# Where the split weights start in their SBUF buffers: byte 128 of a 256-byte period for loaded and narrow tiles

## The chip, the cores and the metric

The kernel runs on one core of a Trainium2 chip. The metric is the device time of one launch in microseconds. Several runs are made and their median is taken; one further execution is recorded by the hardware profiler.

## What is computed

Two layers of an encoder on 256 tokens of width 2048, all in float32. Each layer is a projection with windowed attention and a bidirectional mLSTM behind it, an output projection, and an MLP with a squared ReLU, with RMSNorms around them:

```python
def hybrid_layer(x, ...):
    h = rms_norm(x, g_pre_mix)
    proj = h @ w_in                                   # 2048 x 4624
    aq, ak, av, mq, mk, mv, mo, mg = split(proj)
    att = window_attention(aq, ak, av, attn_sink)     # 8 heads of 128, 2 kv heads
    mem = mlstm_mixer(mq, mk, mv, mo, mg, conv_w, gate_bias, ml_norm_g)
    mix = concatenate([att, mem], axis=-1) @ w_out    # 2048 x 2048
    x = x + rms_norm(mix, g_post_mix)
    h = rms_norm(x, g_pre_mlp)
    u = square(relu(h @ w_up))                        # 2048 x 8192
    x = x + rms_norm(u @ w_down, g_post_mlp)          # 8192 x 2048
    return x
```

Nearly all arithmetic is in the four weight matrices of a layer.

## The kernel before

Every large product is made of three matmuls in the type float32r. Both operands are split into a high part (rounded by ScalarE) and the remainder (VectorE), and the sum is high x high, high x low and low x high. The tokens lie transposed: a tile of `tpool` (names `hT`, `h2T`, `uT`, `attT`, `memT`) holds 8 contraction blocks of 128, each with its high and its low part for 256 tokens, so 2048 bytes a block and partition, 1024 bytes a part.

The weights come from HBM in pieces of 1 MB at most (`load`, line 168). SP issues the DMA into `raw` (line 190), ScalarE makes `whi` (line 191), VectorE makes `wlo` (line 192). `whi` and `wlo` are tiles of the pool `wsp`, four buffers each, of 2048 + 64 elements of four bytes a partition, that is 8448 bytes, 33 times 256. Line 183 sets `o1`, the element of the buffer at which the piece starts.

The weight tiles of a layer are worked off in the order of `STAGES`: ten column tiles of the input projection ("in", widths 512, 512, 512, 272, five of 512, and 256), four of the output projection ("out"), then four blocks (`b` = 0 to 3) of four "up" and four "down" tiles, all 512 columns wide. While a tile is computed, the next one is loaded. There are two ways to compute a tile:

- `mm_k` (line 196), streamed weights: a 128 x 128 block of the tokens is loaded into TensorE as the stationary operand, and 512 (or 272, or 256) columns of weights stream through it. A piece holds four contraction blocks of the tile's width, one behind the other. This is the way of all "in", "out" and "down" tiles and of the first "up" tile of a layer.
- `mm_stationary` (line 259), loaded weights: a 128 x 128 block of weights is loaded, and the 256 tokens of `h2T` stream through it. A piece holds 16 contraction blocks of 128 columns. This is the way of the other 15 "up" tiles of a layer; each is 4 pieces x 16 blocks x 3 matmuls = 192 pairs of a weight load and a matmul. The result is written into the PSUM tile `mms`. The first block of a layer (`b` = 0) has three such tiles in a row, the others four.

TensorE takes its instructions in program order. Between the matmuls of the input projection stand the transposes and small matmuls of attention and mLSTM, which generators hand out one step after each contraction block (`pump`, line 210).

Where things lie in SBUF, as the built program has it (bytes in a partition): the pool `edge` with the 128 and 1024 bytes ahead of it ends at 2048; the four buffers of `tpool` start at 2048, 18432, 34816 and 51200; the buffers of `whi` at 67584, 76032, 84480 and 92928; those of `wlo` at 101376, 109824, 118272 and 126720. All of these are multiples of 256, and so are the starts of all parts in the token tiles. With `o1 = 16` a stationary piece starts 64 bytes behind a multiple of 256; with `o1 = 0` a streamed piece starts at one. The contraction blocks of a stationary piece are 512 bytes long, those of the 512-wide tiles 2048, of the 256-wide tile 1024 and of the 272-wide tile 1088.

Of the kernel before, what the change touches and what calls it, by code (L numbers as in the profile page):

```python
# [75 lines left out]
def stationary(key):  # L76


    _, st, b, n = key
    return st == "up" and (b, n) != (0, 0)  # L80
# [6 lines left out]
def encoder_kernel(ctx, tc, x, wall, rope, conv_w, gate_bias, ml_g, sink, gpre, gpost, out):  # L87
# [70 lines left out]
    order = []  # L158
# [9 lines left out]
    def load(i, begin=None):  # L168


        if i >= len(order) or order[i] in pieces:
            return
        o, w = offs[order[i]]
        k, n = (KC, P) if stationary(order[i]) else (PK, w)
        got = []
        for q in range(NPC):
            raw = wraw.tile([P, k, n], F32, tag="raw", name="raw")
            a = o + q * P * k * n
            src = wall[a:a + P * k * n].rearrange("(p k n) -> p k n", p=P, k=k)
            if begin is not None:  # L180
                begin(q)

            o1 = 16 if stationary(order[i]) else 0
            hi, lo = (
                wsp.tile([P, 2048 + 64], F32R, tag=x, name=f"w{x}")[:, o1:o1 + k * n].rearrange(
                    "p (k n) -> p k n", k=k) for x in ("hi", "lo"))
            step = 1 if begin is not None and q < 2 else k
            for j in range(0, k, step):
                sl = slice(j, j + step)
                nc.sync.dma_start(raw[:, sl], src[:, sl])  # L190
                nc.scalar.activation(hi[:, sl], raw[:, sl], AF.Copy)  # L191
                nc.vector.tensor_tensor(out=lo[:, sl], in0=raw[:, sl], in1=hi[:, sl].bitcast(F32), op=ALU.subtract)  # L192
            got.append((hi, lo))
        pieces[order[i]] = got
# [25 lines left out]
    def mm_tile(key, T, stages=(), after=None, at=None, half=False):  # L220

        load(pos[key])
        load(pos[key] + 1)
        if stages:
            ps = [psmm.tile([P, NT, 512], F32, tag="mm", name="mm")[:, 0] for _ in range(NT)]
# [30 lines left out]
    def mm_stationary(key, T, after):  # L259

        load(pos[key])
        load(pos[key] + 1)
        for pair in range(2):
            both = psmm.tile([P, 2, 512], F32, tag="mm", name="mms")
            ps = both[:, 0].rearrange("p (i t) -> p i t", i=2)
            for i in range(2):
                hi, lo = pieces[key][2 * pair + i]
                for k in range(KC):  # L270
                    Tk = T[k // 8][:, k % 8]
                    nc.tensor.matmul(ps[:, i], lhsT=hi[:, k], rhs=Tk[:, 0], start=(k == 0), stop=False)  # L272
                    nc.tensor.matmul(ps[:, i], lhsT=hi[:, k], rhs=Tk[:, 1], start=False, stop=False)  # L273
                    nc.tensor.matmul(ps[:, i], lhsT=lo[:, k], rhs=Tk[:, 0], start=False, stop=(k == KC - 1))  # L274
            after(pair, ps)
# [369 lines left out]
    def begin(q):  # L645
        if q:
            load_x(1, q - 1)
            load_x(0, q)
# [310 lines left out]
```

## Time and profile before

| | us |
|---|---|
| median of 3 runs | 2143.5 |
| lowest and highest | 2141.52, 2146.43 |
| the profiled execution | 2146.89 |
| its span, first to last instruction | 2145.1 |
| TensorE matmul busy | 2110.1 (98%) |
| TensorE weight load busy | 1868.9 (87%) |
| VectorE busy | 1134.4 (53%) |
| ScalarE busy | 983.8 (46%) |
| GpSimd busy | 60.4 (3%) |

The span is what lies between the first and the last instruction on the chip; the execution's own time has some 2 us around it. Matmuls are pipelined: one starts before the one ahead of it has ended, and the recorded duration of one is longer than what it adds to the time. What it adds is read from the starts in the timeline.

### The profile page before, as it was taken

The numbers are of one execution on the slowest core, as the hardware profiler recorded it, in microseconds if no ns is written. First come the engines' busy times: TensorE is split into PE (matmuls) and PEld (weight loads), VectorE is DVE, ScalarE is ACT, GpSimd is POOL, SyncE is SP. The second block draws the span as 40 slices with busy tenths as digits, with TensorE's granted clock in tenths as the row PEclk, the third lists the DMA queues.
The fourth block names the chain that finished last, engine by engine and source line by source line (L and its number), as shares of the span: only waits on it lengthen the run. The fifth ranks groups of instructions, "written<-read, shape, count | busy, mean of one in ns | idle before, by whom it ended". The sixth has DMA issues, their size and how long they took to land.

```text
span 2145.1 us, 28978 instructions
## 1 busy us (share of the span) xinstructions
PE 2110.1 (98%) x12412; PEld 1868.9 (87%) x12412; DVE 1134.4 (53%) x1219; ACT 983.8 (46%) x1077; POOL 60.4 (3%) x68
## 2 busy tenths in 40 slices
PE   8999999999999999999999999999999999999998
PEld 6878887998998998898878788879889989989986
DVE  6656566544444444444567655575444444444444
ACT  5445544544443353354354555455445434434442
POOL 0000003000000000000020000030000000000000
PEclk9999999999999999999999999999999999999999
DMA  7435354555555555555444344546555555555553
GB/s 257 167 133 174 131 194 167 196 196 193 182 195 190 185 195 188 188 194 190 178 181 160 120 165 148 196 147 223 189 191 194 182 192 195 181 193 195 184 194 118
DMA packets 62209, 388.37 MB, mean 181 GB/s; under 512 B 9600, under 2 KB 10112, under 8 KB 17280
## 3 DMA queue, kind: packets, MB, share of 16 engines
q1 hardware_dynamic: 61936, 386.48, 51.2%
q8 instruction: 97, 1.59, 0.3%
q14 instruction: 32, 0.26, 0.0%
q10 hardware_dynamic: 144, 0.03, 0.0%
HBM read 384.39 MB, written 2.10 MB: 180 GB/s over the span
## 4 chain that ended last, share of the span: by engine, by line
PE 94%; DVE 2%; DMA 1%; ACT 1%; POOL 1%; issue 1%; SPq 0%; POOLq 0%; DVEq 0%; ACTq 0%
PE mm L205 19%; PE mm L203 19%; PE mm L204 19%; PE mms L274 11%; PE mms L272 10%; PE mms L273 10%; DMA raw<-wall 1%; PE pn L594 1%; PE sc L378 1%; PE po L417 1%; DVE xs L792 1%; POOL h2T L325 1%; ACT whi L191 0%; DVE wlo L192 0%; PE cp L577 0%
## 5 line engine op out<-in xcount | busy, mean ns | idle before, releaser
L192 DVE TENSOR_TENSOR wlo<-raw,whi 128x2048 fp32r<-128x2048 f32 (+3 forms) x374 | 828.7, 2217 | 884.5 <-ACT whi L191 884.1
L191 ACT ACTIVATE whi<-raw 128x2048 fp32r<-128x2048 f32 (+3 forms) x374 | 693.2, 1854 | 935.3 <-PE mm L205 511.0
L274 PE MATMUL mms<-h2T,wlo 128*128 128x256 f32 x1920 | 538.8, 281 | 0.0
L272 PE MATMUL mms<-h2T,whi 128*128 128x256 f32 x1920 | 538.6, 281 | 0.0
L273 PE MATMUL mms<-h2T,whi 128*128 128x256 f32 x1920 | 538.6, 281 | 0.0
L203 PE MATMUL mm<-whi,uT 128*128 128x512 f32 x1024 | 398.4, 389 | 0.0
L204 PE MATMUL mm<-wlo,uT 128*128 128x512 f32 x1024 | 398.4, 389 | 0.0
L205 PE MATMUL mm<-whi,uT 128*128 128x512 f32 x1024 | 398.0, 389 | 0.0
L273 PEld LDWEIGHTS mms<-h2T,whi 128*128 128x128 f32 x1920 | 367.1, 191 | 0.3
L274 PEld LDWEIGHTS mms<-h2T,wlo 128*128 128x128 f32 x1920 | 361.2, 188 | 0.0
L272 PEld LDWEIGHTS mms<-h2T,whi 128*128 128x128 f32 x1920 | 360.4, 188 | 0.3
L203 PE MATMUL mm<-whi,hT 128*128 128x512 f32 (+2 forms) x640 | 241.5, 378 | 8.8 <-ACT hT L324 6.5
L205 PE MATMUL mm<-whi,hT 128*128 128x512 f32 (+2 forms) x640 | 241.3, 378 | 1.2 <-POOL hT L325 1.1
L204 PE MATMUL mm<-wlo,hT 128*128 128x512 f32 (+2 forms) x640 | 239.8, 375 | 0.2 <-DVE wlo L192 0.2
L205 PEld LDWEIGHTS mm<-whi,uT 128*128 128x128 f32 x1024 | 192.3, 188 | 40.0
L203 PEld LDWEIGHTS mm<-whi,uT 128*128 128x128 f32 x1024 | 192.3, 188 | 39.6
L204 PEld LDWEIGHTS mm<-wlo,uT 128*128 128x128 f32 x1024 | 192.3, 188 | 39.5
L203 PEld LDWEIGHTS mm<-whi,hT 128*128 128x128 f32 x640 | 121.3, 190 | 29.2 <-ACT hT L324 7.6
L205 PEld LDWEIGHTS mm<-whi,hT 128*128 128x128 f32 x640 | 121.1, 189 | 22.5 <-POOL hT L325 2.0
L204 PEld LDWEIGHTS mm<-wlo,hT 128*128 128x128 f32 x640 | 121.2, 189 | 20.0 <-DVE wlo L192 0.5
L869 DVE SCALAR_TENSOR_TENSOR A_mlp<-mm,s2q,A_mlp 128x512 f32<-128x512 f32 x48 | 34.0, 747 | 37.2 <-PE mm L205 37.2
L203 PE MATMUL mm<-whi,memT 128*128 128x512 f32 x128 | 50.5, 395 | 0.0
(221 smaller groups left out, 1466.1 us busy)
## 6 DMA issues: line engine op xcount, KB each, us to landing
raw<-wall SPq DMA_DIRECT2D x350, 1024.0 KB, 4.8
raw<-wall SPq DMA_DIRECT2D x8, 544.0 KB, 3.5
g<-gpost SPq DMA_DIRECT2D x16, 256.0 KB, 4.6
raw<-wall SPq DMA_DIRECT2D x8, 512.0 KB, 3.3
xs<-x_in SPq DMA_DIRECT2D x8, 256.0 KB, 6.1
raw<-wall SPq DMA_DIRECT2D x8, 256.0 KB, 6.2
y_out<-xs SPq DMA_DIRECT2D x8, 256.0 KB, 2.8
cossin<-rope SPq DMA_DIRECT2D x1, 256.0 KB, 7.1
```

The lines of the kernel that those rows point to most:

```text
L191: nc.scalar.activation(hi[:, sl], raw[:, sl], AF.Copy)
L192: nc.vector.tensor_tensor(out=lo[:, sl], in0=raw[:, sl], in1=hi[:, sl].bitcast(F32), op=ALU.subtract)
L203: nc.tensor.matmul(dst, lhsT=xh, rhs=hi, start=(k == 0), stop=False)
L204: nc.tensor.matmul(dst, lhsT=xh, rhs=lo, start=False, stop=False)
L205: nc.tensor.matmul(dst, lhsT=xl, rhs=hi, start=False, stop=(k == KC - 1))
L272: nc.tensor.matmul(ps[:, i], lhsT=hi[:, k], rhs=Tk[:, 0], start=(k == 0), stop=False)
L273: nc.tensor.matmul(ps[:, i], lhsT=hi[:, k], rhs=Tk[:, 1], start=False, stop=False)
L274: nc.tensor.matmul(ps[:, i], lhsT=lo[:, k], rhs=Tk[:, 0], start=False, stop=(k == KC - 1))
L325: (eng or nc.vector).tensor_tensor(out=lo, in0=ps, in1=hi.bitcast(F32), op=ALU.subtract)
L378: nc.tensor.matmul(sc[:, j], lhsT=qT[:, q0 + j, t * P:(t + 1) * P], rhs=kT[:, g], start=(j == 0), stop=False)
L417: nc.tensor.matmul(po[:, j], lhsT=vA[:, kb, g * HD:(g + 1) * HD], rhs=pT[:, kb], start=(kb == 0), stop=(kb == 1))
L869: nc.vector.scalar_tensor_tensor(out=acc[:, t, sl], in0=ps, scalar=s2[t], in1=acc[:, t, sl], op0=ALU.mult, op1=ALU.add)
```

## The change

The place at which a piece starts in its `whi` and `wlo` buffer changes in two cases. Stationary pieces start at element 32 (128 bytes) instead of 16 (64 bytes). Pieces of the two narrow streamed tiles of a layer (272 and 256 columns, `w < 512`) start at element 32 instead of 0. The 512-wide streamed tiles stay at 0. The number and order of the instructions on every engine and the addresses of all buffers are the same in both programs.

```diff
             if begin is not None:
                 begin(q)
 
-            o1 = 16 if stationary(order[i]) else 0
+
+            o1 = 32 if stationary(order[i]) or w < 512 else 0
             hi, lo = (
                 wsp.tile([P, 2048 + 64], F32R, tag=x, name=f"w{x}")[:, o1:o1 + k * n].rearrange(
                     "p (k n) -> p k n", k=k) for x in ("hi", "lo"))
```

## Rows read from the trace of the kernel before

**Rows 1.** The page: matmul busy time, instructions; granted clock in 40 slices, tenths.

```profile
PE 2110.1 (98%) x12412; PEld 1868.9 (87%) x12412; DVE 1134.4 (53%) x1219; ACT 983.8 (46%) x1077; POOL 60.4 (3%) x68
...
PEclk9999999999999999999999999999999999999999
```

**Rows 2.** The page: the chain that ended last, share of the span by engine.

```profile
PE 94%; DVE 2%; DMA 1%; ACT 1%; POOL 1%; issue 1%; SPq 0%; POOLq 0%; DVEq 0%; ACTq 0%
```

**Rows 3.** The page's groups: line engine op tiles shapes xcount | busy, mean ns | idle before.

```profile
L274 PE MATMUL mms<-h2T,wlo 128*128 128x256 f32 x1920 | 538.8, 281 | 0.0
...
L203 PE MATMUL mm<-whi,uT 128*128 128x512 f32 x1024 | 398.4, 389 | 0.0
```

**Rows 4.** Timeline of matmuls, layer 2, block 1: start us, us, engine line op.

```profile
1602.50 0.28 PE L272 MATMUL mms<-h2T,whi 128*128 128x256 f32 x1
...
1625.11 0.28 PE L272 MATMUL mms<-h2T,whi 128*128 128x256 f32 x1
```

**Rows 5.** Timeline of matmuls, layer 2, block 0: an interruption, two later tile starts.

```profile
1455.03 0.60 PE L843 MATMUL ptu<-ident,ur 128*128 128x128 f32 x4
...
1471.91 0.28 PE L272 MATMUL mms<-h2T,whi 128*128 128x256 f32 x1
...
1493.67 0.28 PE L272 MATMUL mms<-h2T,whi 128*128 128x256 f32 x1
```

**Rows 6.** Timeline of matmuls, the 256-wide streamed tile of layer 2.

```profile
1320.81 0.28 PE L203 MATMUL mm<-whi,hT 128*128 128x256 f32 x1
...
1321.89 0.28 PE L203 MATMUL mm<-whi,hT 128*128 128x256 f32 x1
```

**Rows 7.** Timeline of weight loads (PEld) beside rows 5 and rows 4.

```profile
1471.80 0.19 PEld L272 LDWEIGHTS mms<-h2T,whi 128*128 128x128 f32 x1
1471.91 0.19 PEld L273 LDWEIGHTS mms<-h2T,whi 128*128 128x128 f32 x1
...
1602.50 0.19 PEld L273 LDWEIGHTS mms<-h2T,whi 128*128 128x128 f32 x1
```

**Rows 8.** Groups by line: splits in stretches of loaded (x12), then streamed, weights.

```profile
L191 ACT ACTIVATE whi<-raw 128x2048 fp32r<-128x2048 f32 x12 | 23.0, 1916 | 34.0 <-PE mms L273 34.0
L192 DVE TENSOR_TENSOR wlo<-raw,whi 128x2048 fp32r<-128x2048 f32 x12 | 27.5, 2292 | 36.7 <-ACT whi L191 36.7
...
L191 ACT ACTIVATE whi<-raw 128x2048 fp32r<-128x2048 f32 x14 | 26.9, 1918 | 47.6 <-PE mm L205 47.6
L192 DVE TENSOR_TENSOR wlo<-raw,whi 128x2048 fp32r<-128x2048 f32 x13 | 29.8, 2292 | 32.6 <-ACT whi L191 32.6
```

**Rows 9.** Stretches of stationary blocks: A:B us, PE busy (x), PEld, DVE, ACT, POOL.

```profile
383.70:452.10 68.40, 68.40 (x582) 68.36 (x582) 33.41 (x19) 35.30 (x31) 0.00 (x0) 1.00 0.57 202
539.00:629.60 90.60, 90.60 (x771) 90.56 (x770) 40.89 (x23) 44.05 (x39) 0.00 (x0) 1.00 0.53 187
...
1449.40:1515.50 66.10, 66.10 (x583) 66.06 (x582) 33.41 (x19) 35.27 (x31) 0.00 (x0) 1.00 0.60 208
```

**Rows 10.** The same view of one tile; last: granted clock, DMA share, GB/s.

```profile
1471.91:1493.67 21.76, 21.76 (x194) 21.76 (x193) 11.28 (x7) 11.20 (x10) 0.00 (x0) 1.00 0.58 197
```

**Rows 11.** Timeline of matmuls, a 512-wide "down" tile, 13 starts apart.

```profile
1000.02 0.39 PE L205 MATMUL mm<-whi,uT 128*128 128x512 f32 x1
...
1002.97 0.39 PE L203 MATMUL mm<-whi,uT 128*128 128x512 f32 x1
```

**Rows 12.** Timeline of matmuls, the 272-wide tile: contraction blocks 10 to 13 begin.

```profile
1162.66 0.29 PE L203 MATMUL mm<-whi,hT 128*128 128x272 f32 x1
...
1163.42 0.28 PE L203 MATMUL mm<-whi,hT 128*128 128x272 f32 x1
...
1164.16 0.28 PE L203 MATMUL mm<-whi,hT 128*128 128x272 f32 x1
...
1164.91 0.28 PE L203 MATMUL mm<-whi,hT 128*128 128x272 f32 x1
...
1165.66 0.29 PE L203 MATMUL mm<-whi,hT 128*128 128x272 f32 x1
```

## The prediction

> **What bounds the kernel now.** I read the page first: TensorE is busy for 98% of the span, and its granted clock is at the full level (2.4 GHz) in all 40 slices [rows 1]. The chain that ended last is TensorE work for 94% [rows 2], so a change is worth what it takes off or puts on TensorE's own stream. The groups say what that stream is: some 12,400 pairs of a weight load and a matmul, of which 5760 are the pairs of `mm_stationary` (lines 272 to 274, 1920 each) and most others the 512-wide ones of `mm_k` (lines 203 to 205) [rows 3]. Their mean durations (281 and 389 ns) are no help: matmuls overlap, so what counts is the time from one start to the next, the gap, and that I take from the timeline.
>
> **The gap of one pair.** In the stationary tile that starts at 1602.50 us, the next tile's first matmul starts at 1625.11 [rows 4]: 192 pairs in 22.61 us, 117.8 ns each. In another stationary tile, with the same shapes, the same layer and the same addresses (the tile pools hand out the same buffers), 192 pairs take 1493.67 - 1471.91 = 21.76 us, 113.3 ns each [rows 5]. In the 256-wide streamed tile, where weights and tokens both start at a multiple of 256 bytes, nine pairs take 1321.89 - 1320.81 = 1.08 us, 120.0 ns [rows 6]. All three are pairs of a 128-column load and a 256-column matmul, and TensorE has no idle time in them. They differ by up to 6.7 ns, and what differs between the first and the third is where the operands lie.
>
> The load rows show how a pair runs. In both stationary tiles the next load starts with the running matmul (1602.50 and 1602.50; 1471.91 and 1471.91). The matmul that uses it starts some 0.11 to 0.12 us later [rows 4, 5, 7]. So two reads of SBUF, one for the running matmul and one for the next weights, go on side by side all the time, and the gap is as long as the slower of them. I call the distance the start of the loaded operand less the start of the streamed one, modulo 256 bytes. Stationary tiles have a distance of 64 before and 128 after. The 256-wide tile goes from 0 to 128. The 512-wide tiles stay at 0.
>
> **The change part by part.** No instruction is added, removed or moved: the order on every engine is the same and so is every buffer's address; only the place within the weight buffers moves, by 64 bytes for 30 stationary tiles (15 a layer) and by 128 bytes for two narrow tiles a layer.
>
> *Splitting the weights on ScalarE and VectorE.* They write and read back the moved tiles. At byte 64 (stationary tiles) the 2048-element split takes 1916 ns and 2292 ns, at byte 0 (wide tiles) 1918 and 2292 [rows 8]. The place makes no difference to them: nothing.
>
> *Stationary tiles.* The trace has no pair at distance 128 in which the load is as long as the matmul, so I bound it. From above: 120.0 ns, the gap at distance 0 [rows 6]. From below: 113.3 ns, the gap that the same pairs already reach at times [rows 5]; a little less is possible, since the matmul there starts 0.11 us after its own load has started (1471.80 to 1471.91) [rows 5, 7]. The value that I take is 113.3 ns. The reasons: moving the operands apart from 0 to 64 bytes goes with 2.2 ns less (120.0 to 117.8), so there is a cost in the two reads meeting that depends on the place; and at 64 bytes the pairs run steadily at 117.8 or at 113.3 and never between. The change from the one to the other comes at one place, after four transposes have interrupted the stream at 1455.03 [rows 5]: the addresses stayed, the timing of the two reads against each other was set anew. So 113.3 looks like the pair without a clash, and 117.8 like a clash that the timing either falls into or not. At 128 bytes, as far apart as a period of 256 allows, I expect that the pairs don't fall into it. A straight line through 120.0 and 117.8 would give 115.5, but no stretch of the trace runs at that.
>
> How many pairs gain: the first block of layer 0 (three tiles) takes 68.4 us and each of the six blocks of four tiles some 90.5 (the stretches shown and left out have a slack of 0.1), as 22.61 a tile asks; only the first block of layer 1 takes 66.1, since from the transposes at 1455.03 on its gap is 113.3 [rows 5, 9]. So 27 tiles and the first quarter of one run at 117.8, and each loses 22.61 - 21.76 = 0.85 us: 27.25 x 0.85 = 23.2 us. Nothing else becomes late: in the fast tile TensorE stays busy for all its 21.76 us, with VectorE at 11.28, ScalarE at 11.20 and the DMA engines at 0.58 [rows 10]. Weights arrive in time for the faster pace.
>
> *The 256-wide tile.* Two of them, 96 pairs each, from 120.0 to 113.3 if the forecast holds: 192 x 6.7 ns = 1.3 us at most; transposes and attention work break the run about ten times, so 1.2.
>
> *The 272-wide tile.* Its contraction blocks are 1088 bytes long, so within a piece of four they start at 0, 64, 128 and 192 modulo 256, and after the change at 128, 192, 0 and 64: the same four, in another order. Nothing, whatever a distance costs.
>
> *The 512-wide tiles.* Unchanged at distance 0: 13 gaps in 2.95 us, 226.9 ns [rows 11].
>
> Sum: 23.2 + 1.2 = 24.4 us. The profiled execution took 2146.9 us (span 2145.1), the median of the runs is 2143.5, with 2141.5 to 2146.4 around it; the profiled one is 3.4 us above the median. The gain is the same in both: 2122.5 for such an execution, **2119 us** for the median.
>
> **A rule that speaks against it.** The Trainium skill ("TensorE: Matmul & The Clock Gate", Part 2, the step on LDWEIGHTS) says that TensorE has two independent SBUF read ports, and that loading the next weights takes no bandwidth from the running matmul. By that rule no distance matters and the sum is 0. The three gaps above (113.3, 117.8 and 120.0 ns for one shape) don't agree with a pair whose two reads are independent, but they don't prove that the place is the reason either. The same page (Part 1 and the section on loading) gives 256 / 2.4 + 2.5 = 109.2 ns for the matmul and 128 / 1.2 = 106.7 for the load; by these figures the sum would be an estimated 49 us instead of 24.
>
> **The rivals.**
>
> *The place has nothing to do with it.* The gap is a state that the pairs fall into after a disturbance, and the change leaves it to chance as before. For it: 113.3 and 117.8 stand at the same addresses [rows 4, 5]. Against it: in the eight blocks of stationary tiles the stream enters from other work each time, and only one left the gap of 117.8 [rows 9]; and the 256-wide tile never shows 117.8 over a long run. Time: 2143.5, between 2141 and 2147. This is also what the rule above would give.
>
> *Half of it.* The cost falls in proportion to the distance: 120.0, 117.8, 115.5. Then 27.25 x 192 x 2.3 ns = 12.0 us less, while the tiles that run at 113.3 now lose 2.75 x 192 x 2.2 ns = 1.2: 2143.5 - 10.8 - 0.8 for the narrow tile = 2132.
>
> *Slower: 128 clashes more than 64.* The 272-wide tile is the only place of the trace where the distance runs through all four values. Its blocks of six pairs take 0.76 us where the streamed operand starts at 128 (1162.66 to 1163.42), then 0.74 at 192, 0.75 at 0 and 0.75 at 64 [rows 12]: the block at 128 is, if anything, the slowest. In it the matmul is longer than the load, and the distance changes every six pairs, so no state settles; that is why I give it less weight than the steady tiles. If the stationary pairs go to the 120.0 ns of the worst steady state, a tile takes 23.04 us: 27.25 x 0.43 + 2.75 x 1.28 = 15.2 us more, 2159. It decides from a gap of 117.4 ns on, the present mean: above that the change loses.
>
> *More than forecast.* The load's own 0.11 us becomes the gap: 110 instead of 113.3 ns, 30 x 192 x 3.3 ns = 19 us further, 2100. Nothing in the trace runs at that.
>
> **How the numbers follow.** Forecast (113.3 ns) 0.46; half of it 0.13; no change 0.20; slower 0.17; more 0.04. The limit for a change that can be told from none is 0.2%, 4.3 us. Faster: 0.46 + 0.13 + 0.04 = 0.63; same 0.20; slower 0.17. The range leaves out the slower and the further case, 0.21 less the part of the slower one that stays within a few us, so about 0.2. Its low end is the forecast less the spread of the runs (5 us) and 1 us if the 272-wide tile should gain after all, 2113. Its high end is no change with the bound of 0.2% on top, 2148.
>
> **What the changed profile would show.** Right: the first starts of two neighbouring stationary tiles lie 21.76 us apart instead of 22.61, in all blocks; blocks of four take 87.0 us instead of 90.5; the 256-wide tile runs at 113.3 ns a pair; the 512-wide pairs stay at 226.9; TensorE has no new idle time and the ScalarE and VectorE splits keep their 1.92 and 2.29 us. Half right: the same with 115.5 ns. Wrong: stationary tiles at 22.6 us, in one block or another at 21.8 (the place doesn't matter), or at 23.0 (it clashes more). It would also be wrong if the gap fell but the blocks didn't, because weights came late: then TensorE's idle time before lines 272 to 274, now 0, would show it [rows 3].

## The result, and the profile after

| | us |
|---|---|
| kernel before, median (4 runs) | 2145.0 (2141.5 to 2146.5) |
| changed kernel, median (4 runs) | 2161.2 (2159.8 to 2164.2) |
| ratio, 95% interval | 1.0077 (1.0061 to 1.0093) |
| profiled execution after, span | 2159.8, 2158.0 |

The change costs 16 us (13 to 20 by the interval). The forecast was a gain of 24. In the two profiled executions the spans differ by 2158.0 - 2145.1 = 12.9 us; the one before (2146.9 us) took longer than any of its four runs, the one after was the shortest of its four.

The page after, line by line as in [rows 1 to 3]; all line numbers are higher by one:

```profile
PE 2121.9 (98%) x12412; PEld 1880.5 (87%) x12412; DVE 1134.5 (53%) x1219; ACT 983.6 (46%) x1077; POOL 60.6 (3%) x68
...
PEclk9999999999999999999999999999999999999999
...
PE 94%; DVE 2%; ACT 1%; DMA 1%; POOL 1%; issue 1%; SPq 0%; POOLq 0%; DVEq 0%; ACTq 0%
...
L275 PE MATMUL mms<-h2T,wlo 128*128 128x256 f32 x1920 | 546.1, 284 | 0.0
L274 PE MATMUL mms<-h2T,whi 128*128 128x256 f32 x1920 | 544.4, 284 | 0.0
L273 PE MATMUL mms<-h2T,whi 128*128 128x256 f32 x1920 | 539.7, 281 | 0.0
...
L205 PE MATMUL mm<-wlo,uT 128*128 128x512 f32 x1024 | 398.5, 389 | 0.0
```

The same instructions, the same chain, no idle time before the stationary matmuls, the same mean granted clock to 0.001 (0.995 before, 0.996 after), the same VectorE and ScalarE busy time to 0.2 us. What has grown is the busy time of the stationary matmuls. What they add to the time is in the starts. Timeline of the matmuls after, a stationary tile of layer 2 (the code and the prediction count the layers as 0 and 1), block 1, and the first of the next tile:

```profile
1633.25 0.28 PE L273 MATMUL mms<-h2T,whi 128*128 128x256 f32 x1
1633.37 0.28 PE L274 MATMUL mms<-h2T,whi 128*128 128x256 f32 x1
1633.49 0.28 PE L275 MATMUL mms<-h2T,wlo 128*128 128x256 f32 x1
...
1656.29 0.28 PE L273 MATMUL mms<-h2T,whi 128*128 128x256 f32 x1
```

192 pairs in 23.04 us, 120.0 ns each, where the kernel before had 117.8 [rows 4] and, in one block, 113.3 [rows 5]. The loads still go along with the running matmuls, as in [rows 7]. The stretches of two blocks of three tiles and one of four after (A:B, length, busy time of PE, PEld, DVE, ACT, POOL), beside [rows 9]:

```profile
382.46:451.20 68.74, 68.74 (x581) 68.74 (x579) 33.42 (x19) 35.38 (x31) 0.00 (x0) 1.00 0.57 201
538.39:630.43 92.04, 92.04 (x768) 92.04 (x767) 40.88 (x23) 44.05 (x39) 0.00 (x0) 1.00 0.52 184
1454.28:1523.02 68.74, 68.74 (x581) 68.74 (x580) 33.42 (x19) 35.16 (x31) 0.00 (x0) 1.00 0.58 200
```

A tile in a block of four costs 23.04 - 22.61 = 0.43 us more, 24 of them 10.3 us. The three tiles of layer 2's block 0, of which most ran at 113.3 ns before, take 68.85 us from their first start to the start of the down tile behind them, 65.94 before: 2.9 us more. Those of layer 1 take 68.85 against 68.28: 0.6 us more. Together 13.8 us. The spans differ by 0.9 less: the first stationary tile starts 1.3 us earlier (at 382.46 us, 383.74 before), and 0.3 us more go by between the layers' stationary tiles. In part of the streamed up tile just ahead of it TensorE's granted clock was 1.2 GHz before, and 2.4 after. The same view, before and then after:

```profile
371.50:374.00 2.50, 2.50 (x7) 1.92 (x7) 2.03 (x2) 0.71 (x2) 2.50 (x3) 0.50 0.00 0
...
372.70:375.00 2.30, 2.30 (x14) 1.93 (x13) 1.19 (x1) 0.98 (x1) 2.30 (x2) 1.00 0.00 0
```

The column behind the five engines is the granted clock, 0.50 and 1.00. Just ahead TensorE had waited 1.33 and 0.67 us for `h2T` before, and 1.33 and 0.69 after, so these waits don't tell the two apart.

### The profile page after: what moved, and what is told of

The parts are those of the page before. It is cut to its first block, busy times and chain, and to the rows that moved or that the text cites. A ratio compares the mean times of both kernels' runs of the same rounds, so it can differ in the third digit from the quotient of the medians.

```text
span 2158.0 us, 28978 instructions
## 1 busy us (share of the span) xinstructions
PE 2121.9 (98%) x12412; PEld 1880.5 (87%) x12412; DVE 1134.5 (53%) x1219; ACT 983.6 (46%) x1077; POOL 60.6 (3%) x68
## 4 chain that ended last, share of the span: by engine, by line
PE 94%; DVE 2%; ACT 1%; DMA 1%; POOL 1%; issue 1%; SPq 0%; POOLq 0%; DVEq 0%; ACTq 0%
PE mm L206 19%; PE mm L205 19%; PE mm L204 19%; PE mms L275 11%; PE mms L274 11%; PE mms L273 11%; DMA raw<-wall 1%; PE sc L379 1%; PE pn L595 1%; PE po L418 1%; DVE xs L793 1%; DVE wlo L193 1%; POOL h2T L326 1%; ACT whi L192 0%; PE cp L578 0%
## 5 line engine op out<-in xcount | busy, mean ns | idle before, releaser
L275 PE MATMUL mms<-h2T,wlo 128*128 128x256 f32 x1920 | 546.1, 284 | 0.0
L206 PEld LDWEIGHTS mm<-whi,hT 128*128 128x128 f32 x640 | 120.8, 189 | 22.8 <-POOL hT L326 2.4
```

Source lines behind the costliest of these rows:

```text
L206: nc.tensor.matmul(dst, lhsT=xl, rhs=hi, start=False, stop=(k == KC - 1))
```

## The experiments

**Which half of the change costs.** One kernel with the stationary half alone, one with the narrow half alone:

```diff
-            o1 = 16 if stationary(order[i]) else 0
+            o1 = 32 if stationary(order[i]) else 0
```

> Only the stationary half of the change: loaded weights at byte 128, the narrow streamed tiles at 0 as before. If the loss is that of the stationary pairs, the time is that of the changed kernel, some 16 us above the kernel before (2161), with 22.9 us a tile. If it came from the narrow tiles: no difference (2145).

```diff
-            o1 = 16 if stationary(order[i]) else 0
+            o1 = 16 if stationary(order[i]) else 32 if w < 512 else 0
```

> Only the narrow half: the 272- and 256-wide streamed tiles at byte 128, loaded weights at 64 as before. If the loss is that of the stationary pairs: within 1 us of the kernel before, with a gap of about 118.5 ns in the 256-wide tile in place of 120 (0.3 us over both). If it came from the narrow tiles: 2161.

The stationary half took 2159.2 us, 1.0078 (1.0063 to 1.0093) times the kernel before: the whole loss. The narrow half took 2144.4, 0.9999 (0.9987 to 1.0011). In its trace the mean of 170 gaps of the 256-wide tiles (those not broken by other work) is 118.7 ns instead of 119.8, 0.2 us in all, and that of the 272-wide tiles 125.4 instead of 125.2. Both as expected.

**Does the place matter, and is it the distance?** A table gives each stationary tile and each 512-wide down tile its own place, in steps of 16 bytes, upwards in layer 1 and downwards in layer 2. A second kernel has the same table and moves tokens and weights together by 128 bytes, with a pad at the start of the pool `edge`:

```diff
+SWEEP = {}
+for _st in ("up", "down"):
+    _tiles = [(b, n) for b in range(4) for n in range(4) if (_st, b, n) != ("up", 0, 0)]
+    for _i, (_b, _n) in enumerate(_tiles):
+        SWEEP[0, _st, _b, _n] = 4 * _i
+        SWEEP[1, _st, _b, _n] = 60 - 4 * _i
...
-            o1 = 16 if stationary(order[i]) else 0
+            o1 = SWEEP.get(order[i], 0)
```

> Every stationary tile of a layer starts its pieces at another place: tile 0 at byte 0, the next at 16, 32 and so on to 224 in layer 1; in layer 2 from 240 down to 16. The sixteen 512-wide down tiles of a layer do the same (0 to 240, and 240 to 0). Theory A (the distance of the two operands modulo 256 sets the gap): both layers give the same gap at the same place; 117.8 ns at 64 and 120 at 128, as in the two kernels known; the least gap is some other place's, perhaps 113.3 ns. Theory B (the timing of the two reads at a tile's entry sets it, the place doesn't): no curve, the two layers differ at the same place by several ns, values of 113.3, 117.8 and 120 are strewn about. On the 512-wide tiles, A expects gaps between 216 and 232 ns that repeat in both layers, B 226.7 everywhere.

> The same sweep, with the token tiles and the weight buffers both moved by 128 bytes, so that each tile has the same distance as in the sweep without that, but both operands lie 128 bytes elsewhere. Theory A (the distance sets the gap): the same gap tile by tile, 117.8 ns at a distance of 64, 120 at 128. Theory C (the loaded operand's own place modulo 256 sets it): the curve is moved by 128 bytes, so the tile at a distance of 192 shows the 117.8 ns that byte 64 showed. Theory B (entry timing alone): no agreement tile by tile.

The mean gap in ns of each tile, worked out from its last 91 gaps (stationary) or 75 (down tiles), by the place of the piece in bytes (4 x `o1`):

| place | stationary, layer 1 | layer 2 | 512-wide, layer 1 | layer 2 |
|---|---|---|---|---|
| 0 | 120.0 | | 226.7 | 226.7 |
| 16 | 118.3 | 118.4 | 231.6 | 231.6 |
| 32 | 118.4 | 118.3 | 233.3 | 233.3 |
| 48 | 117.8 | 117.8 | 233.4 | 230.0 |
| 64 | 113.3 | 113.3 | 228.9 | 228.9 |
| 80 | 118.8 | 118.8 | 231.1 | 231.1 |
| 96 | 117.3 | 117.3 | 233.3 | 233.3 |
| 112 | 120.0 | 120.0 | 231.1 | 226.7 |
| 128 | 118.7 | 120.0 | 232.3 | 233.4 |
| 144 | 120.0 | 120.0 | 233.3 | 233.3 |
| 160 | 119.9 | 120.0 | 234.2 | 234.3 |
| 176 | 118.1 | 118.1 | 233.3 | 233.3 |
| 192 | 113.3 | 117.8 | 233.3 | 233.3 |
| 208 | 116.7 | 116.7 | 234.7 | 234.7 |
| 224 | 116.7 | 116.6 | 233.4 | 233.3 |
| 240 | | 120.0 | 226.7 | 236.6 |

(For a stationary tile this is the place of the loaded operand, and so the distance as the prediction defines it. For a down tile it is the place of the streamed operand, and the distance is 256 less the place.) With both operands moved by 128 bytes, 60 of these 62 values come back within 0.1 ns; the two that don't are the first two tiles of layer 2's block 0 (place 240: 117.4 instead of 120.0, and 224: 117.8 instead of 116.6), of which the first is interrupted by the transposes. Three tiles of the timeline show it: those at 64, at 128 and at 144, each from its first matmul to the next tile's first; first without the move:

```profile
565.18 0.28 PE L280 MATMUL mms<-h2T,whi 128*128 128x256 f32 x1
...
586.95 0.28 PE L280 MATMUL mms<-h2T,whi 128*128 128x256 f32 x1
...
744.09 0.28 PE L280 MATMUL mms<-h2T,whi 128*128 128x256 f32 x1
...
766.87 0.28 PE L280 MATMUL mms<-h2T,whi 128*128 128x256 f32 x1
...
789.91 0.29 PE L280 MATMUL mms<-h2T,whi 128*128 128x256 f32 x1
```

and with both operands moved by 128 bytes:

```profile
565.56 0.28 PE L281 MATMUL mms<-h2T,whi 128*128 128x256 f32 x1
...
587.33 0.28 PE L281 MATMUL mms<-h2T,whi 128*128 128x256 f32 x1
...
744.47 0.28 PE L281 MATMUL mms<-h2T,whi 128*128 128x256 f32 x1
...
767.25 0.28 PE L281 MATMUL mms<-h2T,whi 128*128 128x256 f32 x1
...
790.29 0.29 PE L281 MATMUL mms<-h2T,whi 128*128 128x256 f32 x1
```

21.77, 22.78 and 23.04 us in both. So what counts is the distance of the two operands and not the place of the loaded one (theory A; theory C would have moved the curve by 128 bytes, and the curve is not the same 128 bytes on: 118.3 at 16, 120.0 at 144). But the curve is not the one that the prediction drew. For stationary tiles it has two lows, at 64 and at 192 (where layer 2 shows 117.8, with 116.7 and 116.6 at 208 and 224), and 128 lies on the ridge between them, about as bad as 0. The kernel before stood in one of the lows. And theory B has a part in it: the two layers differ in stationary tiles at 128 and 192 and in 512-wide ones at 48, 112, 128 and 240, at the same place and with other tiles ahead.

**Finer steps.** The same with steps of 4 bytes around both lows, and 0 to 124 for the down tiles (`FINE` takes the place of `SWEEP`):

```diff
+for _i in range(15):
+    _b, _n = divmod(_i + 1, 4)
+    FINE[0, "up", _b, _n] = 9 + _i
+    FINE[1, "up", _b, _n] = 41 + _i
+for _i in range(16):
+    _b, _n = divmod(_i, 4)
+    FINE[0, "down", _b, _n] = _i
+    FINE[1, "down", _b, _n] = 16 + _i
```

> A sweep in steps of 4 bytes: stationary tiles of layer 1 at bytes 36 to 92, of layer 2 at 164 to 220; the 512-wide down tiles of layer 1 at bytes 0 to 60, of layer 2 at 64 to 124. If the clash is between lines or banks of 64 bytes, the gap changes smoothly or in few steps, with the least of 113.3 near 64 and 192, and no place below it; the 512-wide tiles have no gap under 226.7. If 113.3 and 226.7 are only the best of a coarse grid, some place shows less, down to the 216 ns that 512 columns would need (half the 427 of a stretch at the lower clock level is 213).

No stationary tile went below 113.3 and no 512-wide one below 226.7 (at 0; up to 240.0 at 100 and 116). But the gap isn't smooth: 113.3 came at 52, 64, 76 and 88, with 117.7, 119.5, 118.3 and 118.3 at the four places 56, 60, 68 and 72, and in layer 2 the tile at 192 showed 117.8. One tile, at 48, ran at 123.3, though 48 gave 117.8 in both layers of the coarser sweep. The expectation of a low at 64 and 192 with smooth sides was wrong. What ran before a tile has a part in its gap, as the entries below show, and a table of places alone can't tell the two apart.

**Do the two reads meet at all?** This kernel leaves out the products of blocks 1 to 3 of each layer. In blocks 1 of both layers every weight load reads one column over and over (`to_broadcast`), in blocks 2 every matmul streams one, in blocks 3 both; stationary tiles at 128 as in the changed kernel:

```diff
+ONE = {(0, 1): (True, False), (0, 2): (False, True), (0, 3): (True, True),
+       (1, 1): (True, False), (1, 2): (False, True), (1, 3): (True, True)}
...
+        if w1:
+            xh, xl = (a[:, 0:1].to_broadcast([P, P]) for a in (xh, xl))
+        if t1:
+            hi, lo = (a[:, 0:1].to_broadcast([P, w]) for a in (hi, lo))
...
+                    wh, wl = (a[:, k, 0:1].to_broadcast([P, P]) if w1 else a[:, k] for a in (hi, lo))
+                    th, tl = (Tk[:, j, 0:1].to_broadcast([P, SEQ]) if t1 else Tk[:, j] for j in range(2))
```

> Measures the clash by itself, loaded weights at byte 128, the rest as before: in block 1 of both layers every weight load reads one column again and again instead of 128 (the place in SBUF stands still, the instruction is as long), in block 2 every matmul streams one column again and again, in block 3 both. The products of those blocks are left out of the computation in this sense. It is done for the stationary up tiles and for the 512-wide down tiles. If the two reads meet in SBUF (theory A), the stationary gap falls from 120 ns to 113.3 or less in blocks 1 and 2 and stays at 119 to 120 in block 0; the 512-wide gap falls from 226.7 towards 216. If the gap is the array's own (load and matmul through the same array, no matter what is read), nothing changes: 120 and 226.7 in all blocks.

Timeline of its matmuls, two starts 192 pairs apart in each: stationary in block 0 of layer 2 (nothing taken away), in block 1 and in block 2 of layer 1:

```profile
1460.78 0.28 PE L284 MATMUL mms<-h2T,whi 128*128 128x256 f32 x1
...
1483.56 0.28 PE L284 MATMUL mms<-h2T,whi 128*128 128x256 f32 x1
...
565.41 0.28 PE L284 MATMUL mms<-h2T,whi 128*128 128x256 f32 x1
...
587.81 0.28 PE L284 MATMUL mms<-h2T,whi 128*128 128x256 f32 x1
...
743.01 0.28 PE L284 MATMUL mms<-h2T,whi 128*128 128x256 f32 x1
...
764.45 0.28 PE L284 MATMUL mms<-h2T,whi 128*128 128x256 f32 x1
```

and 512-wide, two starts 96 pairs apart, in the down tiles of blocks 0, 1 and 2 of layer 1:

```profile
494.73 0.39 PE L212 MATMUL mm<-whi,uT 128*128 128x512 f32 x1
...
516.49 0.39 PE L212 MATMUL mm<-whi,uT 128*128 128x512 f32 x1
...
677.09 0.40 PE L212 MATMUL mm<-whi,uT 128*128 128x512 f32 x1
...
699.33 0.40 PE L212 MATMUL mm<-whi,uT 128*128 128x512 f32 x1
...
828.10 0.38 PE L212 MATMUL mm<-whi,uT 128*128 128x512 f32 x1
...
848.86 0.38 PE L212 MATMUL mm<-whi,uT 128*128 128x512 f32 x1
```

The stationary gap is 118.6 ns with both operands walking, 116.7 where the load stands still and 111.7 where the stream does; the 512-wide gap 226.7, 231.7 and 216.3. With both standing still they are 111.7 and 216.3 again. So the two reads do meet: with the stream as it was, another way of reading the load alone moves the gap, from 118.6 to 116.7 and from 226.7 to 231.7. A stream that stands still saves 10.4 ns a pair in the 512-wide tiles, and between 1.6 ns (of 113.3) and 8.3 (of 120.0) in the stationary ones. How much of that saving is due to the load isn't shown: no run has a walking stream with no load beside it. A load that stands still doesn't free the stream; in the wide tiles it costs more than one that walks at distance 0. The expectation had that wrong: it takes a stream that stands still, not a load that does.

**What sets 113.3 or 117.8 at the distance 64.** All stationary pieces lie at 64 as before, but the first piece of a block, 48 pairs, lies elsewhere:

```diff
+ENTRY = {(0, 0): 12, (0, 1): 12, (0, 2): 0, (0, 3): 8, (1, 0): 0, (1, 1): 20, (1, 2): 32, (1, 3): 48}
...
+    first = n == (1 if b == 0 else 0) and q == 0
+    return ENTRY[l, b] if first else 16
```

> All stationary pieces lie at byte 64 as before, but the first piece (48 pairs) of the first stationary tile of each block lies elsewhere: in layer 1 at 48, 48, 0 and 32 (blocks 0 to 3), in layer 2 at 0, 80, 128 and 192. In the sweep the tile at 64 ran at 113.3 ns where it followed one at 48 and at 117.8 where it was the first of its block in the kernel before. Theory D (two steady rhythms at the same distance, chosen by what ran just before): blocks whose first piece lies at 48 run at 113.3 ns afterwards, some others too, the rest at 117.8; a block keeps its rhythm to its end. Theory E (the distance alone fixes the gap, and the 113.3 of the sweep had another reason, such as the wide tiles' places): all blocks at 117.8 but those that were at 113.3 in the kernel before.

Behind a first piece at 32, 128 and 192 bytes the rest of the block runs at 113.3 ns, all its tiles to the end; behind 0 and 48 (twice each) and 80 at 117.8. Tile starts of the block entered at 48 (block 1) and of the one entered at 32 in layer 1:

```profile
540.50 0.28 PE L283 MATMUL mms<-h2T,whi 128*128 128x256 f32 x1
...
563.14 0.28 PE L283 MATMUL mms<-h2T,whi 128*128 128x256 f32 x1
...
585.75 0.28 PE L283 MATMUL mms<-h2T,whi 128*128 128x256 f32 x1
...
917.67 0.28 PE L283 MATMUL mms<-h2T,whi 128*128 128x256 f32 x1
...
939.43 0.28 PE L283 MATMUL mms<-h2T,whi 128*128 128x256 f32 x1
```

Behind the first tile, 22.61 and 21.76 us a tile, with the same addresses. So there are two steady rhythms at this distance, and what ran just before chooses (theory D). That an entry at 48 leads to 113.3, which the sweep had suggested, was wrong: there a whole tile at 48 came first. Block 0 ran at 117.8 in both layers here, at 113.3 in both layers of the kernel with the narrow half alone and in one of the kernel before, though its stationary tiles lie at the same addresses in the last two. In those two the pairs run at 117.8 up to the four transposes that interrupt the first tile, and change to 113.3, where they do, right behind them. Why they do so in one case and not in another isn't shown. It is worth some 2.3 us a layer, about half of the 5 us between the shortest and the longest run of the kernel before.

**Has 128 a better rhythm too?** The same for the changed kernel: the rest at 128, first pieces at six other places (64 and 192 twice each, 0, 32, 48 and 96).

```diff
+ENTRY = {(0, 0): 16, (0, 1): 16, (0, 2): 0, (0, 3): 8, (1, 0): 48, (1, 1): 24, (1, 2): 12, (1, 3): 48}
...
+    return ENTRY[l, b] if first else 32
```

> All stationary pieces at byte 128 as in the changed kernel, but the first piece of each block elsewhere: at 64, 64, 0 and 32 in layer 1, at 192, 96, 48 and 192 in layer 2. If 128 is worse by its place: the rest of every block at one of the gaps already seen there, 118.7 or 120.0 ns, whatever came first. If 128 also has a rhythm of 113.3 ns that the changed kernel only failed to enter: some blocks show it.

Tile starts of layer 2, block 1 (entered at 96) and block 2 (entered at 48):

```profile
1634.14 0.28 PE L283 MATMUL mms<-h2T,whi 128*128 128x256 f32 x1
...
1657.18 0.28 PE L283 MATMUL mms<-h2T,whi 128*128 128x256 f32 x1
...
1813.10 0.28 PE L283 MATMUL mms<-h2T,whi 128*128 128x256 f32 x1
...
1835.88 0.28 PE L283 MATMUL mms<-h2T,whi 128*128 128x256 f32 x1
```

Seven blocks run at 118.7 ns, the one entered at 96 at 120.0; none at 113.3 (2158.5 us in one run). With these six entries the loss at 128 is that of the place, with two rhythms of its own, both above the 117.8 of the kernel before.

**A kernel that enters 113.3 everywhere.**

```diff
+def start(key, q):
+    l, st, b, n = key
+    if not stationary(key):
+        return 0
+    entry = (n, q) == ((0, 0) if b else (1, 1))
+    return 48 if entry else 16
...
-            o1 = 16 if stationary(order[i]) else 0
+            o1 = start(order[i], q)
```

> All stationary pieces at byte 64, but one piece of 48 pairs in each block at 192: the first of the block in blocks 1 to 3, the second of the first tile in block 0 (behind the transposes that interrupt that tile). Theory D (the rhythm is chosen by what ran just before): all six blocks of four tiles run at 113.3 ns, as the one block entered at 192 did, 87.3 us a block instead of 90.5; block 0 probably too, 65.6 to 66.1 us instead of 68.4 in layer 1. Sum: six times 3.2 us and 2.5 us, some 20 us less than the kernel before, 2124. If the one block was luck of its place in the program: some blocks at 117.8, and a gain of 5 to 15 us.

It took 2126.3 us (2125.9 to 2129.7, 5 runs) against 2145.6 for the kernel before, run alongside: 0.9914 (0.9899 to 0.9929), 19 us faster than the kernel before and 35 faster than the change. Stretches of its block 0 and block 1 in layer 1, then in layer 2, as in [rows 9]:

```profile
385.90:451.72 65.82, 65.82 (x580) 65.81 (x579) 33.41 (x19) 35.30 (x31) 0.00 (x0) 1.00 0.59 209
538.90:626.06 87.16, 87.16 (x769) 87.16 (x768) 40.89 (x23) 44.17 (x39) 0.00 (x0) 1.00 0.55 194
...
1438.39:1504.43 66.04, 66.04 (x581) 66.03 (x579) 33.41 (x19) 35.23 (x31) 0.00 (x0) 1.00 0.59 208
1591.61:1678.76 87.15, 87.15 (x768) 87.15 (x767) 40.89 (x23) 44.17 (x39) 0.00 (x0) 1.00 0.54 194
```

All 30 stationary tiles end at 113.3 ns. With entries at 32 in layer 1 and at 128 in layer 2 instead:

> As the kernel with entries at 192, with the one piece at 32 in layer 1 and at 128 in layer 2. Theory D: again 113.3 ns in the six blocks of four tiles, with an entry that costs about as much (21.9 to 22.0 us for the first tile of a block).

2127.9 us in one run: 113.3 in the six blocks of four and in layer 2's block 0, 117.8 in layer 1's. The first tile of a block of four, with the entry in it, takes 21.99 (192), 22.00 (32) or 22.09 us (128) to the next tile's first matmul, against 21.76 for one without.

## Why the prediction was wrong, point by point

*What bounds the kernel, and what doesn't change:* right. TensorE's stream is the whole of it; VectorE and ScalarE kept their busy time, no wait appeared, the 512-wide down pairs stayed at 226.7 ns, and the 272-wide tiles moved by 0.2 ns. One reading was too coarse: a 9 in the clock row [rows 1] stands for 90% or more, and the clock was not at its full level throughout, as the stretch at 0.50 above shows. It cost about 1 us of the comparison, and none of the mechanism.

*That the distance of the two operands matters:* right, and shown by the two sweeps, which agree with the operands moved together. It held against the rule on two independent read ports that the prediction weighed from the Trainium skill ("TensorE: Matmul & The Clock Gate", Part 2, the step on LDWEIGHTS): here the gap of a 256-wide pair goes from 113.3 to 120.0 ns with the distance, and that of a 512-wide one from 226.7 to 231.7 when the load alone reads one column over and over, so the load is not without cost to the running matmul.

*The value for the stationary pairs at 128:* here it failed. The bounds were 113.3 and 120.0; the prediction took the lower end, and the measured value is the upper: 120.0 in the blocks of four, 118.7 in block 0. The reason given was that the cost falls as the operands move apart, and that 128 is as far apart as a period of 256 allows. Two points, 120.0 at 0 and 117.8 at 64, fixed neither the period nor the shape. The sweep has lows at 64 and 192 and a ridge at 112 to 160. The term of 23.2 us became -13.8.

*That 113.3 is the pair without a clash, which another place would give:* half right. 113.3 is close to the 111.7 of a stream that stands still. But at 64 it is one of two rhythms of that distance, which the next pairs keep; it was no sign of what a larger distance would bring. The row that showed it at unchanged addresses [rows 5] said that there was something to gain without moving the tiles away from 64, and that is what the last kernel does: 19 us, of the 23.2 that the same row had been counted for.

*The rivals:* the one that came true, 128 clashing more than 64, was given 0.17 and a time of 2159; it came out at 2161, with the price that it named (23.04 us a tile). The evidence quoted for it, 0.76 us for six pairs at 128 in the 272-wide tile [rows 12], was set aside as unsettled, since the distance changes there every six pairs. It was the only row that had the distance in question, and one block of six pairs was too little to read from it: 0.76 against 0.75 at 0 is the last digit. All undisturbed gaps of the two 272-wide tiles of the kernel before, 44 to 46 for each place, average 125.8 ns at 0, 125.1 at 64, 125.8 at 128 and 123.9 at 192. So the trace before already had 128 as slow as 0, with less at 64 and 192.

*The narrow 256-wide tile:* expected a gain of 1.2 us, measured 0.2 (118.7 instead of 113.3 ns): the same mistake on a small scale.

## What to carry to other kernels

Where a gap between instructions takes several steady values at the same addresses, the lower one is there to be entered, and a short piece ahead with another layout may do it; look at what ran just before, not only at the place. Two measured points of an effect that may be periodic are no slope: sweep the place inside one kernel, tile by tile, which costs one run. A place of the trace that has the very value in question, however disturbed, deserves the mean of all its gaps before a line is drawn through other values.

## What the runs showed of the hardware

- In float32r pairs the streamed operand and the weight load beside it get in each other's way. Without a walking stream a 512-wide pair takes 216.3 ns and a 256-wide one 111.7; with one, 226.7 to 240.0 and 113.3 to 120.0 (two tiles of the fine sweep had 120.8 and 123.3), depending on the distance of the two start addresses and on what ran before.
- Of the two places it is the distance that counts: moving both by 128 bytes, the one move that was tried, leaves 60 of 62 tiles as they were.
- The pairs settle into rhythms that last through tile borders to the end of a block, some 90 us, where other work follows. At 64 bytes two were seen, 113.3 and 117.8 ns, at 128 also two, 118.7 and 120.0. Why a given entry leads to a given rhythm, and how SBUF is arranged that the lows lie at 64 and 192, stays open: no run here looks at that.
- The 512-wide pairs, over half of the time, were nowhere better than the 226.7 ns that they have at distance 0. Their 10.4 ns a pair were not got rid of, and other entries weren't tried for them.
